# A hybrid decoder step: fetches of the next K block issued one by one on SP, odd sample states in two steps with B masked

## Chip, cores and metric

The kernel runs on one core of a Trainium2 chip. The metric is the device time of one execution in microseconds, the median of several runs. Engines are called PE (matmul), DVE (vector), ACT (scalar), POOL (GpSimd) and SP (sync); PEld is PE's weight load.

## What is computed

One inference step of a two-layer decoder for a prompt of 1024 + 16 positions and 8 samples of 4 positions, 1072 columns in all. Layer 0 is a linear-attention mixer, layer 1 a Mamba-2 mixer; each is followed by a SwiGLU feed-forward (FFN). The parts that the change touches are the FFN, and the new states of the samples in layer 1:

```python
def swiglu(x, w_gate, w_up, w_down):
    return (jax.nn.silu(x @ w_gate) * (x @ w_up)) @ w_down

# ssd_scan, state of one sample: decay, then the sum over its 4 positions
u = jnp.einsum('bnjgrp,bnjgs->bngrps', xdt * decay_end[..., None], bc)
s = chunk_decay[..., None, None] * s + u      # (32 heads x 64) x 128 per sample
```

## The kernel before

**Number format.** Every operand is split in a high and a low part, and a product is three matmuls (wh·xh, wl·xh, wh·xl; `mm3`, lines 229 to 234). Activations lie as 8 rows of 128 features in `xh` and `xl`, 1072 columns each.

**FFN in quads.** Three of the 22 gate/up tiles are done plainly. The other 19 go through `quad_gu`: a two-by-two block product in seven products ("forms" a11, s1, s2, s4, s3, a12, a22), each form 24 matmuls of 268 columns. The results are combined on DVE, split and stored to DRAM tensor `fd` by POOL's queue (`store`, L408 and L409); two quads make a pair, and the second (odd) one combines and stores most. Buffers `t` for this come from a ring of ten. The last quad (number 21) is stored by SP to `oh` and `ol` (`spill`).

The down product (`quad_down`) goes over five K blocks, `DOWN = (2, 2, 2, 2, 1)`. In one block four quads (p = 0 to 3) run over the seven forms; with n = 2 a form is 12 matmuls, so a block is 336. The right operands of a block are 7 forms x n pieces of 536 KB, fetched back from `fd` (L577): forms 0 to 3 into rows of `xh` and `xl` of the block's parity, forms 4 to 6 into strips of the arena (`fo`). The 29 strips of the arena are handed out first in, first out.

**Weights.** `W.pump` keeps up to six forms ready ahead of their use. A raw tile of 512 KB (`raw`, two buffers) comes on SP's queue (L71); a form is summed on DVE where needed (L97), copied high on ACT (L115) and its low part taken on DVE (L116). DVE also adds the finished products into `acc` (L503), in the order of its queue.

**Fetches.** `fetch(c + 1)` stands at the start of block c, all 14 pieces in a row on POOL's queue; block 0 is fetched while quad 21 runs, by the hook `last_gu`. In `quad_gu` and `quad_down` the hook runs before `W.pump(RING)`.

**Samples.** The samples' new states are a side task (`Driver`, `D.add`), stepped between the forms of `quad_gu` at `RATE[7]` = 0.6 steps per form: `even_samples` in layer 0 (32 steps), `odd_samples` in layer 1 (32 states, two steps each). For a state, `odd_samples` loads it on SP (L1533), masks the 512 columns of x for the sample (L1535, DVE), decays the state (L1537, DVE), and one step later multiplies (L1540, PE), adds (L1541, DVE) and stores on SP (L1542). There are two state buffers, halves of one strip. The side task holds four strips until it ends.

A scheduler places the recorded instructions on the engines' queues; within a queue they then run in order.

Of the kernel before, what the change touches and what calls it, by code (L numbers as in the profile page):

```python
# [162 lines left out]
class Core:  # L163
# [247 lines left out]
    def quad_gu(self, W, i, hook=None):  # L411
# [47 lines left out]
        for f in FORMS:  # L459
            w, = W.take(1)  # L460
            for tb in range(2):
                ps = self.product(bank, f, w, self.right, 4, tb)
                if f == "a11":
                    nc.scalar.activation(out=part(keep, 0, tb), in_=ps, func=AF.Copy)
                elif f == "s1":
                    add(part(keep, 2, tb), ps, part(keep, 0, tb))
                elif f == "s2":
                    s2[tb] = self.tmp(Q)
                    add(s2[tb], ps, part(keep, 0, tb))
                elif f == "s4":  # L470
                    sg[tb] = self.tmp(Q)
                    add(sg[tb], ps, s2[tb])
                    nc.scalar.activation(out=sg[tb], in_=sg[tb], func=AF.Silu)
                elif f == "s3":
                    second(ps, tb)
                elif f == "a12":
                    sg[tb] = self.tmp(Q)
                    nc.scalar.activation(out=sg[tb], in_=ps, func=AF.Silu)  # L478
                else:
                    first(ps, tb)  # L480
            self.drop(*w[2])
            if hook:
                hook(f)
            W.pump(RING)
            yield

    def quad_down(self, W, right, n, p, acc, ap1, c, hook=None):
# [7 lines left out]
        for f in FORMS:  # L495
            w, = W.take(1)
            for tb in range(2):
# [4 lines left out]
                else:  # L502
                    nc.vector.tensor_tensor(out=a, in0=a, in1=ps, op=ALU.add)  # L503
            self.drop(*w[2])
            if hook:
                hook(f)
            W.pump(RING)
# [29 lines left out]
    def ffn(self, W, side, order=(0, 1, 2)):  # L537
# [17 lines left out]
                    W.pump(RING)  # L555
        D.drain()
        self.pstags = ["kt", "sc"]
        D.add(self.later, RATE[7])

        nc = self.nc  # L560
        start = [sum(DOWN[:c]) for c in range(len(DOWN))]
        F, own = [[None] * 7 for _ in DOWN], [[] for _ in DOWN]

        def fetch(c, forms=range(7)):


            for f in forms:
                F[c][f] = []
                for j in range(DOWN[c]):
                    if f < 4:  # L570
                        r = 4 * j + f
                        x = (self.xh, self.xl)[r // 4][:, 2 * (r % 4) + c % 2]
                    else:
                        own[c].append(self.strip(F32R, "fo"))
                        x = own[c][-1].t
                    F[c][f].append(x)
# [7 lines left out]

        def last_gu(f):
            if f == "a11":
                fetch(0, range(4))
            elif f == "s2":
                self.drop(*self.T[0], *self.T[1])
                fetch(0, range(4, 7))  # L590

        for i in range(PLAIN, 22):
            yield from self.quad_gu(W, i, last_gu if i == 21 else None)
# [5 lines left out]
        end = len(DOWN) - 1  # L599
        rows = range(1 - end % 2, KD, 2)  # L600
        for c, n in enumerate(DOWN):
            if c < end:
                fetch(c + 1)
            else:
# [494 lines left out]
    def even(self, W, side):  # L1099
# [111 lines left out]
            self.drop(*u)  # L1211
        self.nps = 8
        W.pump(4)
        self.later = self.even_samples(prs)


    def odd_units(self):
# [305 lines left out]
    def odd_samples(self, grs):  # L1523
# [4 lines left out]
        for gr in grs:  # L1528
            g = gr.g
            bs, xs = self.bst(g)  # L1530
            for s in range(8):
                S0 = sp.t[:, (s % 2) * 512:(s % 2) * 512 + 512]
                nc.sync.dma_start(out=S0, in_=I["ss_in"][:, s, 512 * g:512 * g + 512])  # L1533
                xm = self.bxs[2].t[:, 512:1024]
                nc.vector.tensor_scalar(out=xm[:96], in0=xs[:96].bitcast(F32), scalar1=self.onehot[:, s:s + 1],  # L1535
                                        scalar2=None, op0=ALU.mult)
                nc.vector.tensor_tensor(out=v8(S0), in0=v8(S0), in1=gr.cd[:, :, s:s + 1].to_broadcast([P, 8, 64]), op=ALU.mult)  # L1537
                yield
                bu = self.ps(512)
                nc.tensor.matmul(bu, lhsT=bs[:96], rhs=xm[:96], start=True, stop=True)  # L1540
                nc.vector.tensor_tensor(out=S0, in0=S0, in1=bu, op=ALU.add)  # L1541
                nc.sync.dma_start(out=O["ss_s"][:, s, 512 * g:512 * g + 512], in_=S0)  # L1542
                yield
        self.drop(sp, *self.bxs)

    def sgate(self, gr):
# [36 lines left out]
    def odd(self, W, side):  # L1583
# [87 lines left out]
            self.drop(*u)  # L1671
        self.nps = 8
        W.pump(4)
        self.later = self.odd_samples(grs)

    def ffn_units(self, l):
        g, u, d = (self.I[f"{n}{l}"] for n in ("wg", "wu", "wd"))
# [16 lines left out]
ODD0 = 6  # L1694
NPS = 7
START = 6
RATE = [1.2, 1.2, 1.5, 1.5, 1.5, 6.5, 6.0, 0.6, 1.25]


class Driver:  # L1700
# [207 lines left out]
```

## Time and profile before

| | us |
|---|---|
| median of 3 runs | 3062.77 |
| lowest, highest | 3062.67, 3066.0 |
| the profiled execution | 3070.39 |
| its span, first to last instruction | 3068.6 |
| PE busy in the span | 2895.4 (94%) |
| PEld | 2770.4 (90%) |
| DVE | 2246.9 (73%) |
| ACT | 1402.8 (46%) |
| POOL | 360.2 (12%) |

PE's busy share is that of pipelined instructions, so the number of matmuls in a stretch says more than its busy time. In time from the span's start: layer 0 has its gate/up quads from about 680 to 1080 us and the down product to about 1300; layer 1 has them from about 2330 to 2758 and 2758 to 2985.

### The profile page before, as it was taken

To read this page: it belongs to the slowest core of one execution; us is meant where nothing else is said; L and a number is where in the kernel's file an instruction comes from. 1 tells how busy PE (TensorE), PEld (TensorE's weight loads), DVE (VectorE), ACT (ScalarE), POOL (GpSimd) and SP (SyncE) were. 2 spreads that over 40 slices of the span, in tenths; PEclk is the share of its full clock that TensorE was granted. 3 is DMA by queue.
4 is the path that set the end of the run, shared out by engine and by line. 5 is a ranking of instruction groups with operands and counts; after the bars stand their busy time and mean duration, and the time that the engine had idled before them with its cause. 6 is when DMAs were issued, how large, how long until landed. Compare 5 with 4: busy or idle time off the path is not lost. (4 is left out here: it accounts for less than half of the span.)

```text
span 3068.6 us, 54657 instructions
## 1 busy us (share of the span) xinstructions
PE 2895.4 (94%) x20386; PEld 2770.4 (90%) x20386; DVE 2246.9 (73%) x4977; ACT 1402.8 (46%) x3195; POOL 360.2 (12%) x693
## 2 busy tenths in 40 slices
PE   7999999999999988997999999999999999998986
PEld 7998989999899988987889898989999999998986
DVE  7645545687887757897877777775478888874887
ACT  5533435553344442245767575854354343343213
POOL 0000000002333331100000000000001333342100
PEclk9999999999999999998999999999999999999998
DMA  4121226234454485443344445366333655558534
GB/s 137 45 66 35 77 69 203 96 106 148 155 161 143 138 304 222 143 121 102 95 124 129 137 128 135 119 207 211 140 132 112 190 176 171 178 179 316 177 115 129
DMA packets 246267, 442.79 MB, mean 144 GB/s; under 512 B 36177, under 2 KB 172273, under 8 KB 246001
## 3 DMA queue, kind: packets, MB, share of 16 engines
q1 hardware_dynamic: 201360, 292.16, 30.6%
q0 software_dynamic: 44640, 147.14, 13.6%
q8 instruction: 160, 2.62, 0.4%
q14 instruction: 107, 0.87, 0.1%
HBM read 295.12 MB, written 144.07 MB: 143 GB/s over the span
## 5 line engine op out<-in xcount | busy, mean ns | idle before, releaser
L232 PE MATMUL ps<-xh,wh 128*128 128x384 f32 (+1 forms) x2520 | 842.4, 336 | 18.7 <-ACT xh L248 7.6
L233 PE MATMUL ps<-xh,wl 128*128 128x384 f32 (+1 forms) x2520 | 832.5, 331 | 8.6 <-DVE wl L130 8.6
L234 PE MATMUL ps<-xl,wh 128*128 128x384 f32 (+1 forms) x2520 | 832.7, 331 | 0.0
L232 PEld LDWEIGHTS ps<-xh,wh 128*128 128x128 f32 x2520 | 480.5, 191 | 42.2 <-issue 12.3
L233 PEld LDWEIGHTS ps<-xh,wl 128*128 128x128 f32 x2520 | 481.1, 191 | 14.9 <-DVE wl L130 10.2
L234 PEld LDWEIGHTS ps<-xl,wh 128*128 128x128 f32 x2520 | 480.3, 191 | 3.9 <-issue 1.9
L408 POOL DMA_DIRECT2D fd<-t x252 | 137.0, 544 | 1185.8 <-ACT t L248 810.9
L115 ACT ACTIVATE w_s<-sums 128x512 fp32r<-128x512 f32 (+2 forms) x292 | 146.4, 514 | 279.9 <-DVE sums L97 183.7
L115 ACT ACTIVATE w_a<-raw 128x512 fp32r<-128x512 f32 (+2 forms) x214 | 106.8, 515 | 235.4 <-DMA raw<-in_wd 74.5
L232 PE MATMUL qa<-xh,w_a 128*128 128x268 f32 x688 | 200.3, 291 | 5.3 <-ACT t L478 5.0
L130 DVE TENSOR_TENSOR wl<-raw,wh 128x1024 fp32r<-128x1024 f32 (+1 forms) x113 | 138.1, 1223 | 85.2 <-ACT wh L129 71.4
L233 PE MATMUL qa<-xh,w_a 128*128 128x268 f32 x688 | 199.1, 289 | 0.0
L234 PE MATMUL qa<-xl,w_a 128*128 128x268 f32 x672 | 193.7, 288 | 0.0
L248 ACT ACTIVATE t<-t 128x268 fp32r<-128x268 f32 (+2 forms) x230 | 99.8, 438 | 189.2 <-DVE t L419 94.4
L232 PE MATMUL qb<-t,w_s 128*128 128x268 f32 x608 | 174.9, 288 | 9.8 <-DVE t L419 9.8
L233 PE MATMUL qb<-t,w_s 128*128 128x268 f32 x608 | 173.9, 286 | 0.0
L234 PE MATMUL qb<-t,w_s 128*128 128x268 f32 x608 | 173.7, 286 | 0.0
L129 ACT ACTIVATE wh<-raw 128x1024 fp32r<-128x1024 f32 (+1 forms) x113 | 119.3, 1056 | 111.9 <-DMA raw<-in_wd 29.1
L116 DVE TENSOR_TENSOR w_s<-sums,w_s 128x512 fp32r<-128x512 f32 (+2 forms) x292 | 155.8, 544 | 15.8 <-ACT w_s L115 4.0
L97 DVE TENSOR_TENSOR sums<-raw 128x512 f32<-128x512 f32 (+2 forms) x156 | 83.3, 535 | 111.2 <-DMA raw<-in_wd 63.9
L409 POOL DMA_DIRECT2D fd<-t x252 | 137.0, 543 | 34.2 <-DVE t L249 8.9
L116 DVE TENSOR_TENSOR w_a<-raw,w_a 128x512 fp32r<-128x512 f32 (+2 forms) x214 | 116.0, 550 | 32.8 <-ACT w_a L115 27.0
(404 smaller groups left out, 7541.9 us busy)
## 6 DMA issues: line engine op xcount, KB each, us to landing
fd<-t POOLq DMA_DIRECT2D x504, 134.0 KB, 3.0
fo<-fd POOLq DMA_DIRECT2D x54, 536.0 KB, 11.1
raw<-in_wg SPq DMA_DIRECT2D x44, 512.0 KB, 4.0
raw<-in_wu SPq DMA_DIRECT2D x44, 512.0 KB, 4.7
xh<-fd POOLq DMA_DIRECT2D x40, 536.0 KB, 7.2
raw<-in_wd SPq DMA_DIRECT2D x40, 512.0 KB, 4.3
xl<-fd POOLq DMA_DIRECT2D x32, 536.0 KB, 8.8
cumb<-cum_d SPq DMA_DIRECT2D x32, 512.0 KB, 5.7
```

The lines of the kernel that those rows point to most:

```text
L97: nc.vector.tensor_tensor(out=sums[f], in0=x, in1=y, op=op)
L115: nc.scalar.activation(out=tiled(hi), in_=src, func=AF.Copy)
L116: nc.vector.tensor_tensor(out=tiled(lo), in0=src, in1=tiled(hi).bitcast(F32), op=ALU.subtract)
L129: c.nc.scalar.activation(out=hi.t[:, :w], in_=r, func=AF.Copy)
L130: c.nc.vector.tensor_tensor(out=lo.t[:, :w], in0=r, in1=hi.t[:, :w].bitcast(F32), op=ALU.subtract)
L232: nc.tensor.matmul(out, lhsT=wh, rhs=xh, start=first, stop=False, **kw)
L233: nc.tensor.matmul(out, lhsT=wl, rhs=xh, start=False, stop=False, **kw)
L234: nc.tensor.matmul(out, lhsT=wh, rhs=xl, start=False, stop=last, **kw)
L248: self.nc.scalar.activation(out=hi, in_=src, func=AF.Copy)
L408: self.nc.gpsimd.dma_start(out=self.fd[:, i, FORMS.index(f), o:o + Q], in_=hi.bitcast(F32))
L409: self.nc.gpsimd.dma_start(out=self.fd[:, i, FORMS.index(f), 2 * Q + o:2 * Q + o + Q], in_=lo.bitcast(F32))
```

## The change

1. In `quad_gu` and `quad_down` `W.pump(RING)` now stands ahead of the hook.
2. `fetch` issues one piece on SP's queue (`nc.sync`) in place of POOL's. In block c a hook `paced` runs after every form and issues one piece of block c + 1 every second form (every fourth where the next block has seven pieces; in the last block one pair of plain rows every seventh). For block 0 the first eight pieces still go out at once after form a11 of quad 21, the other six after s2.
3. `even_samples` are stepped at 0.3 per form, `odd_samples` at 0.55.
4. `odd_samples` loads the state and masks B (128 columns in four slots) one step ahead of its product; decay, addition and store come a step later. Load and store are on POOL's queue.

```diff
@@ quad_gu and quad_down
             self.drop(*w[2])
+            W.pump(RING)
             if hook:
                 hook(f)
-            W.pump(RING)
             yield
@@ ffn
-        D.add(self.later, RATE[7])
+        D.add(*self.later)
...
+        pieces = lambda c: [(f, j) for f in range(7) for j in range(DOWN[c])]
...
-                    nc.gpsimd.dma_start(out=x.bitcast(F32), in_=self.fd[:, start[c] + j, f])
+            nc.sync.dma_start(out=x.bitcast(F32), in_=self.fd[:, start[c] + j, f])
+
+        def fetch_plain(i):
+            for dst, src in ((self.xh, self.oh), (self.xl, self.ol)):
+                nc.sync.dma_start(out=dst[:, rows[i]].bitcast(F32), in_=src[:, i])
...
         for c, n in enumerate(DOWN):
-            if c < end:
-                fetch(c + 1)
-            else:
-                for i, r in enumerate(rows):
-                    for dst, src in ((self.xh, self.oh), (self.xl, self.ol)):
-                        nc.gpsimd.dma_start(out=dst[:, r].bitcast(F32), in_=src[:, i])
+            todo = [(fetch, c + 1, *x) for x in pieces(c + 1)] if c < end else [(fetch_plain, i) for i in range(PLAIN + 1)]
+            every, count = 4 * 7 // len(todo), [0]
+
+            def paced(f):
+                count[0] += 1
+                if todo and count[0] % every == 0:
+                    fn, *args = todo.pop(0)
+                    fn(*args)
+
             for p in range(4):
-                yield from self.quad_down(W, right(c), n, p, acc, ap1, c)
+                yield from self.quad_down(W, right(c), n, p, acc, ap1, c, paced)
             self.drop(*own[c])
@@ odd_samples
+        masked = lambda i: self.bxs[2].t[:, 512 + (i % 4) * P:512 + (i % 4) * P + P]
+        def load(i):
+            gr, s = steps[i]
+            nc.gpsimd.dma_start(out=state(i), in_=I["ss_in"][:, s, 512 * gr.g:512 * gr.g + 512])
+            nc.vector.tensor_scalar(out=masked(i)[:96], in0=self.bst(gr.g)[0][:96].bitcast(F32),
+                                    scalar1=self.onehot[:, s:s + 1], scalar2=None, op0=ALU.mult)
+        def product(i):
+            bu[i] = self.ps(512)
+            nc.tensor.matmul(bu[i], lhsT=masked(i)[:96], rhs=self.bst(steps[i][0].g)[1][:96], start=True, stop=True)
+        load(0)
+        yield
+        for i, (gr, s) in enumerate(steps):
+            S0 = state(i)
+            if i + 1 < len(steps):
+                load(i + 1)
+            product(i)
+            yield
+            nc.vector.tensor_tensor(out=v8(S0), in0=v8(S0), in1=gr.cd[:, :, s:s + 1].to_broadcast([P, 8, 64]), op=ALU.mult)
+            nc.vector.tensor_tensor(out=S0, in0=S0, in1=bu[i], op=ALU.add)
+            nc.gpsimd.dma_start(out=O["ss_s"][:, s, 512 * gr.g:512 * gr.g + 512], in_=S0)
+            yield
@@
-RATE = [1.2, 1.2, 1.5, 1.5, 1.5, 6.5, 6.0, 0.6, 1.25]
+RATE = [1.2, 1.2, 1.5, 1.5, 1.5, 6.5, 6.0, 0.3, 1.25, 0.55]
```

**SP in the down product of layer 1.** Before, from the stores of the last gate/up quad (`oh`, `ol`) on, with `raw` the raw weight tiles:

```order
L627 DMA ol<-t 128x268
L71 DMA raw<-in_wd 128x4x256
L626 DMA oh<-t 128x268
L627 DMA ol<-t 128x268
L71 DMA raw<-in_wd 128x4x256 x13
L71 DMA raw<-in_wd 128x2x256 x4
```

In the change, on the same queue, from the raw tile of quad p = 2 of block 0 on:

```order
L71 DMA raw<-in_wd 128x4x256
L577 DMA xh<-fd 128x1072
L577 DMA xl<-fd 128x1072
L577 DMA xh<-fd 128x1072
L71 DMA raw<-in_wd 128x4x256
L577 DMA xl<-fd 128x1072
L577 DMA xh<-fd 128x1072
L577 DMA xl<-fd 128x1072
L577 DMA xh<-fd 128x1072
L71 DMA raw<-in_wd 128x4x256
L577 DMA xl<-fd 128x1072
L577 DMA fo<-fd 128x1072 x2
```

The pieces that stood on POOL's queue now stand on SP's, three or four between two raw tiles.

**The sample states of layer 1.** Before, their loads (`ssm<-in_ss_in`) and stores (`out_ss_s<-ssm`) stand on SP among the raw gate and up tiles:

```order
L1533 DMA ssm<-in_ss_in 128x512
L1542 DMA out_ss_s<-ssm 128x512
L1533 DMA ssm<-in_ss_in 128x512
L71 DMA raw<-in_wg 128x1024
L71 DMA raw<-in_wu 128x1024
L1542 DMA out_ss_s<-ssm 128x512
```

In the change they stand on POOL, among the stores of the quads' results (L408, L409):

```order
L1560 DMA out_ss_s<-ssm 128x512
L408 DMA fd<-t 128x268
L409 DMA fd<-t 128x268
L408 DMA fd<-t 128x268
L409 DMA fd<-t 128x268
L1542 DMA ssm<-in_ss_in 128x512
L408 DMA fd<-t 128x268 x2
L409 DMA fd<-t 128x268 x2
L1560 DMA out_ss_s<-ssm 128x512
L1542 DMA ssm<-in_ss_in 128x512
```

They moved from the weights' queue to that of the results; a load stands right behind the store of the state before it, or some results later.

**DVE in the gate/up quads of layer 1.** Before, with the mask (L1535), the decay (L1537) and the addition (L1541) of a sample state among the quad's own work:

```order
L1541 TENSOR_TENSOR ssm<-ssm,ps 128x512
L419 TENSOR_TENSOR hraw<-hraw,t 128x268
L116 TENSOR_TENSOR w_s_27451<-sums,w_s_27451 128x512
L1535 TENSOR_SCALAR bxs<-bxs,c_onehot 96x512
L116 TENSOR_TENSOR w_s_27487<-sums,w_s_27487 128x512
```

In the change, in a like place:

```order
L1558 TENSOR_TENSOR ssm<-ssm,cd_19874 128x512
L419 TENSOR_TENSOR t<-qb,keep 128x268
L97 TENSOR_TENSOR sums<-raw 128x512
L97 TENSOR_TENSOR sums<-sums,raw 128x512
L419 TENSOR_TENSOR t<-qb,keep 128x268
L116 TENSOR_TENSOR w_s_27959<-sums,w_s_27959 128x512
L1559 TENSOR_TENSOR ssm<-ssm,ps 128x512
L419 TENSOR_TENSOR t<-qe,t 128x268
L97 TENSOR_TENSOR sums<-raw,sums 128x512
L1543 TENSOR_SCALAR bxs<-bxs,c_onehot 96x128
```

The mask is now 96x128, and decay and addition follow each other within one step.

## Rows read from the trace of the kernel before

**Rows 1.** busy us (instructions) of each engine by stretch, columns in its first line

```profile
core 0: us, PE busy (x) PEld busy (x) DVE busy (x) ACT busy (x) POOL busy (x), PEclk, DMA share, GB/s
2770.00:2780.00 10.00, 4.21 (x32) 3.78 (x31) 0.00 (x0) 0.00 (x0) 3.24 (x6) 0.89 1.04 411
2780.00:2800.00 20.00, 16.91 (x119) 16.91 (x120) 10.15 (x29) 10.30 (x29) 3.25 (x6) 0.80 0.96 372
2800.00:2820.00 20.00, 20.00 (x164) 20.00 (x164) 10.90 (x29) 10.41 (x31) 5.96 (x11) 1.00 0.56 196
2820.00:2840.00 20.00, 15.02 (x110) 14.81 (x109) 12.26 (x36) 3.67 (x10) 1.62 (x3) 0.91 0.70 268
2840.00:2860.00 20.00, 20.00 (x165) 20.00 (x164) 18.03 (x50) 4.94 (x14) 1.96 (x4) 1.00 0.22 64
2860.00:2880.00 20.00, 15.84 (x128) 15.65 (x127) 11.95 (x33) 3.88 (x11) 5.62 (x11) 1.00 1.03 388
```

**Rows 2.** the same view, three stretches of layer 0

```profile
1100.00:1120.00 20.00, 11.28 (x74) 10.30 (x73) 7.43 (x22) 5.88 (x17) 6.56 (x13) 0.80 1.04 412
1160.00:1180.00 20.00, 15.84 (x111) 15.63 (x110) 14.54 (x40) 4.07 (x11) 0.00 (x0) 0.83 0.47 173
1200.00:1220.00 20.00, 16.04 (x118) 15.85 (x117) 13.83 (x41) 4.65 (x12) 2.19 (x5) 0.91 0.82 312
```

**Rows 3.** chain that ended last, 2756 to 2870: start, us, what

```profile
2765.97 14.18 DMA raw<-in_wd
...
2865.93 12.08 DMA raw<-in_wd
```

**Rows 4.** timeline of DVE: start, us, instruction, idle time before it

```profile
2780.25 0.42 DVE L97 TENSOR_TENSOR sums<-raw 128x256 f32<-128x256 f32 x1 [10.71 <-DMA raw<-in_wd]
```

**Rows 5.** DMA queues, 2758 to 2800: packets, MB, share of 16 engines

```profile
q0 software_dynamic: 3621, 13.76, 81.2%
q1 hardware_dynamic: 2736, 2.67, 18.3%
```

**Rows 6.** the view of rows 1, where SP alone issues large fetches

```profile
2052.00:2056.00 4.00, 4.00 (x24) 3.34 (x22) 1.43 (x3) 3.95 (x11) 0.00 (x0) 1.00 1.07 388
```

**Rows 7.** page, part 6: DMA issues over the whole span

```profile
fd<-t POOLq DMA_DIRECT2D x504, 134.0 KB, 3.0
...
raw<-in_wd SPq DMA_DIRECT2D x40, 512.0 KB, 4.3
```

**Rows 8.** that view: layer 0 with samples, without, layer 1 with

```profile
680.00:880.00 200.00, 184.67 (x1447) 181.51 (x1446) 164.79 (x332) 75.08 (x169) 60.63 (x112) 0.99 0.49 157
880.00:1060.00 180.00, 180.00 (x1455) 179.58 (x1454) 146.70 (x317) 77.36 (x173) 63.04 (x117) 1.00 0.46 142
2320.00:2700.00 380.00, 356.68 (x2781) 349.50 (x2779) 320.90 (x688) 148.50 (x330) 114.86 (x212) 1.00 0.53 170
```

**Rows 9.** that view: an odd unit of layer 0 without samples

```profile
950.00:960.00 10.00, 10.00 (x82) 9.90 (x81) 9.81 (x25) 6.25 (x15) 7.06 (x13) 1.00 0.60 181
```

**Rows 10.** waits of PE, 2320 to 2758: us in total, times, longest

```profile
PE qb L232 <- DVE t L419: 19.5, 15, 2.0
```

**Rows 11.** groups of DVE instructions, 2320 to 2758: busy us, mean ns, idle

```profile
L1537 DVE TENSOR_TENSOR ssm<-ssm,cd 128x512 f32<-128x512 f32 x32 | 22.0, 688 | 11.7 <-DMA ssm<-in_ss_in 11.5
L1541 DVE TENSOR_TENSOR ssm<-ssm,ps 128x512 f32<-128x512 f32 x32 | 21.7, 678 | 0.0
L1535 DVE TENSOR_SCALAR bxs<-bxs,c_onehot 96x512 fp32r<-96x512 f32 x31 | 14.8, 476 | 0.0
```

**Rows 12.** DMA issues, 2320 to 2758, columns as above

```profile
ssm<-in_ss_in SPq DMA_DIRECT2D x32, 256.0 KB, 2.8
out_ss_s<-ssm SPq DMA_DIRECT2D x32, 256.0 KB, 2.2
```

**Rows 13.** page, part 5: busy us, mean ns, idle before

```profile
L408 POOL DMA_DIRECT2D fd<-t x252 | 137.0, 544 | 1185.8 <-ACT t L248 810.9
```

**Rows 14.** waits, 2320 to 2740

```profile
DVE t L249 <- DMA fd<-t: 6.4, 8, 1.5
```

More of the change, by code (lines that the diff above doesn't have):

```diff
@@ L504, in quad_down @@
             self.drop(*w[2])
+            W.pump(RING)
             if hook:
                 hook(f)
-            W.pump(RING)
             yield
@@ L557, in ffn, with fetch @@
         self.pstags = ["kt", "sc"]
-        D.add(self.later, RATE[7])
+        D.add(*self.later)
         nc = self.nc
         start = [sum(DOWN[:c]) for c in range(len(DOWN))]
[L562 to L572, printed above, removed]
-                    else:
-                        own[c].append(self.strip(F32R, "fo"))
-                        x = own[c][-1].t
-                    F[c][f].append(x)
-                    nc.gpsimd.dma_start(out=x.bitcast(F32), in_=self.fd[:, start[c] + j, f])
+        F, own = [[[] for _ in range(7)] for _ in DOWN], [[] for _ in DOWN]
+        end = len(DOWN) - 1
+        rows = range(1 - end % 2, KD, 2)
+        pieces = lambda c: [(f, j) for f in range(7) for j in range(DOWN[c])]
+        def fetch(c, f, j):
+            if f < 4:
+                r = 4 * j + f
+                x = (self.xh, self.xl)[r // 4][:, 2 * (r % 4) + c % 2]
+            else:
+                own[c].append(self.strip(F32R, "fo"))
+                x = own[c][-1].t
+            F[c][f].append(x)
+            nc.sync.dma_start(out=x.bitcast(F32), in_=self.fd[:, start[c] + j, f])
+        def fetch_plain(i):
+            for dst, src in ((self.xh, self.oh), (self.xl, self.ol)):
+                nc.sync.dma_start(out=dst[:, rows[i]].bitcast(F32), in_=src[:, i])
         def right(c):
@@ L586, in last_gu @@
             if f == "a11":
-                fetch(0, range(4))
+                for f, j in pieces(0)[:8]:
+                    fetch(0, f, j)
             elif f == "s2":
                 self.drop(*self.T[0], *self.T[1])
-                fetch(0, range(4, 7))
+                for f, j in pieces(0)[8:]:
+                    fetch(0, f, j)
         for i in range(PLAIN, 22):
@@ L598, in ffn @@
         ap1 = [self.strip(F32, "ap1") for _ in range(2)]
-        end = len(DOWN) - 1
-        rows = range(1 - end % 2, KD, 2)
         for c, n in enumerate(DOWN):
-            if c < end:
-                fetch(c + 1)
-            else:
-                for i, r in enumerate(rows):
-                    for dst, src in ((self.xh, self.oh), (self.xl, self.ol)):
-                        nc.gpsimd.dma_start(out=dst[:, r].bitcast(F32), in_=src[:, i])
+            todo = [(fetch, c + 1, *x) for x in pieces(c + 1)] if c < end else [(fetch_plain, i) for i in range(PLAIN + 1)]
[5 more added lines that the diff above has]
+                    fn(*args)
             for p in range(4):
-                yield from self.quad_down(W, right(c), n, p, acc, ap1, c)
+                yield from self.quad_down(W, right(c), n, p, acc, ap1, c, paced)
             self.drop(*own[c])
@@ L1213, in even @@
         W.pump(4)
-        self.later = self.even_samples(prs)
+        self.later = self.even_samples(prs), RATE[7]
     def odd_units(self):
@@ L1527, in odd_samples @@
         v8 = lambda a: a.rearrange("p (h d) -> p h d", h=8)
[L1528 to L1543, printed above, removed]
+        steps = [(gr, s) for gr in grs for s in range(8)]
+        state = lambda i: sp.t[:, (i % 2) * 512:(i % 2) * 512 + 512]
+        masked = lambda i: self.bxs[2].t[:, 512 + (i % 4) * P:512 + (i % 4) * P + P]
+        bu = [None] * len(steps)
+        def load(i):
[18 more added lines that the diff above has]
+            yield
         self.drop(sp, *self.bxs)
@@ L1673, in odd @@
         W.pump(4)
-        self.later = self.odd_samples(grs)
+        self.later = self.odd_samples(grs), RATE[9]
     def ffn_units(self, l):
```

## The prediction

> **What bounds the kernel now.** PE does, nearly everywhere: busy 94% of the span. So I looked for stretches in which PE does fewer matmuls than its full pace, and asked what it waited for there. I read the busy time by stretch first, then the chain that ended last, then the DMA queues of the worst stretch, then the groups and waits of the gate/up stage.
>
> *Down product.* Full pace is 164 matmuls in 20 us (the stretch from 2800 in [rows 1]), 8.2 per us. Layer 1 falls short by 50 in the ten us from 2770, by 45 from 2780, by 54 from 2820 and by 36 from 2860: 185 matmuls, 22.6 us. Layer 0 falls short by 90, 53 and 46 [rows 2]: 189, or 23.0 us. Together 45.6 us. Part of each loss is idle PE, part a lower granted clock behind the stop (0.89 and 0.80 in [rows 1]). The chain says who is late: a raw weight tile, 14.18 and 12.08 us from issue to landing [rows 3], where the median is 4.3 [rows 7]. DVE stood 10.71 us in front of a sum for it [rows 4]; the additions of finished products queue behind that sum on DVE, so PE's banks are not freed and PE stops. Why the tile is late: the DMA engines were full (403 to 412 GB/s in the bad stretches of [rows 1, 2]), and 13.76 MB of 16.4 were the fetches and stores on POOL's queue, which took 81.2% of the time; SP's queue got 18.3% [rows 5]. All pieces of a block go out at once, and the weights starve for some 20 us.
>
> *Gate/up quads.* Layer 0 without samples does 1455 matmuls in 180 us, 8.08 per us, PE never idle. With samples it does 1447 in 200 us [rows 8]: 170 short, 21 us; 2 us of that are the 16 sample products themselves (one long matmul is worth about two short ones), so 19 us are stalls. Layer 1 does 2781 in 380 us: 291 short, 36 us; about 4 are the 32 sample products and an estimated 3 the longer matmuls of plain tiles at its start, so 29 us are stalls. PE waits there for DVE's reading of a bank, 19.5 us in 15 waits [rows 10]. DVE is the cause: an odd unit holds it 9.81 us of ten even without samples [rows 9].
>
> **The change, part by part.** Sums are against the profiled execution, 3070.39 us (span 3068.6 and 1.8 around it). The median of the runs is 3062.77, so at the end I scale by 3062.77/3070.39 = 0.9975.
>
> *Fetches on SP, spaced.* A block of 336 matmuls lasts 41.0 us at full pace, a form 1.46 us. It needs 14 pieces of 0.549 MB and 4 raw tiles of 0.524 MB: 9.8 MB, 239 GB/s, where SP's queue alone has moved 388 [rows 6]. Bandwidth suffices, if the weights get theirs in time. At 388 GB/s a piece takes 1.41 us. What stands before a raw tile on SP is now three or four pieces, by the order shown ahead. SP does not space these itself: it issues them as soon as their buffers are free. But the tile in front of them waits for DVE to free its raw buffer, once per quad (10.2 us), so a group of four goes out at once, takes 5.6 us, and is through before the next tile is issued. That tile then lands in about 4.3 us. It is needed seven to eight forms after its issue (10.2 to 11.7 us): it is issued when the a22 form of its buffer's quad is made, six forms ahead of PE. Even a tile that stands right behind four pieces lands within 5.6 + 4.3 = 9.9 us. So I expect the stalls to go, apart from the start of block 0, where 14 pieces and eight stores stand before the tile for p = 2. There the fetch begins right after PE's a11 of quad 21, no longer behind POOL's own stores, but so it now runs beside quad 20's stores, whose `t` buffers come back later. I leave 3 us per layer for that: of 45.6 us, 40 go. The ends are 15 (a late tile in each quad, below) and 45. What is late next is DVE: at PE's full pace it is busy 18.03 us of 20 in block 1 (the stretch from 2840 in [rows 1]), so it can follow, with little to spare. Strips give no wait: a `fo` strip handed out was last read some eight forms earlier. POOL loses 126 issues and nobody waited for POOL's time there. `W.pump` ahead of the hook puts a raw tile ahead of a piece: at most one piece, 1.41 us, on a path with slack, taken as nothing.
>
> *Samples of layer 1.* DVE spent 22.0 + 21.7 + 14.8 us on them and stood 11.7 us for the loads [rows 11]: 70 us. The new mask has a quarter of the columns: between 119 ns (a quarter of 476) and 476; I take 250, near the middle. That is 32 x (688 + 678 + 250) ns = 52 us, and the load, issued one step (1.8 forms, 5.3 us) ahead, lands in 2.8 us [rows 12], so the wait goes. 52 for 70 us: if stalls follow DVE's load, 29 x 18/70 = 7 us go; if only load beyond some slack stalls PE, all 29. Since DVE has almost no slack in an odd unit [rows 9] I stay near the low end and take 8, and 3 more because SP no longer waits for sample data in front of raw tiles.
>
> *POOL takes the samples' DMAs.* 64 more issues of 0.54 us [rows 13] stand among the results' stores. A load waits until the store before it in the same buffer has landed (2.2 us, [rows 12]; 3.0 for POOL's own, [rows 7]), and the results queued behind it hold their `t` buffers; DVE already waits 6.4 us for these [rows 14]. Nothing, if each falls between stores; up to 31 x (2.2 + 1.1) = 102 us if every one holds all. Mostly the load stands with no ready store behind it. I take 5 us: half of 1.1 us in each of nine odd units.
>
> *Samples of layer 0.* Same work over twice the time. Proportional stalls: 0 gained; stalls from excess alone: up to 19. I take 3. Their four strips are held 55 forms longer, which costs a form of lead that is hidden now.
>
> Sum: -40 - 8 - 3 + 5 - 3 = -49. 3070.4 - 49 = 3021.4, times 0.9975: **3014 us**.
>
> **Rivals.** *Gate/up stalls mostly vanish.* Half the sample density in layer 0 and a third less in layer 1 stay under DVE's room: 43 + 22 + 10 = 75 us gone, 2995, scaled 2988. For it: without samples there is no stall at all [rows 8]. Against: 9.81 of ten.
>
> *The spacing isn't one.* Since only a raw tile's wait holds SP, a group goes out at once, and a tile may land 9.9 us after issue plus some 2 us by which DVE lags. Against a lead of 10.2 to 11.7 that is late by 0 to 2 us in each of the 28 quads of full blocks: 28 x 1.1 = 31 of the 45.6 us stay. With 9 from the samples: 3070.4 - 24 = 3046, scaled 3039. For it: the fetch is as large as before. The Trainium skill ("DMA: Bandwidth & Descriptors", section "Queues, rings and completion order") says that a DMA engine takes turns between queue rows packet by packet, and that on one row descriptors start in order. By that rule the move costs the weights the turns of a row of their own, which is what this rival prices; the trace shows how little those turns gave, 18.3% [rows 5]. The same page, section "Issuing engines are not separate DMA queues", says that issuing from another engine saves only the time to issue. By that, the queue alone would change nothing (3063), and all of the gain lies in the spacing; the full DMA engines in [rows 1] agree.
>
> *Slower: POOL is held.* In layer 1's gate/up quads a sample load waits on POOL for the landing of a store, results queue behind it, the ten `t` buffers run out, and DVE and then PE stop. With the share s of the 102 us that reaches PE the sum is -54 + 102 s: break-even at s = 0.53, slower than the median by over 0.2% from s = 0.59, and 3111 at s = 1. For it: [rows 14], and loads that stand directly behind a store. Against: where load and store are neighbours, the results behind them belong to later forms.
>
> **How the numbers follow.** Forecast (3014) 0.58; stalls vanish (2988) 0.14; no real spacing (3039) 0.15; POOL held 0.13, of which 0.05 within 0.2% and 0.08 slower. 0.2% (6 us) is about what a measurement of this kernel can tell from no change. Faster 0.87, same 0.05, slower 0.08. The range reaches to both faster cases, with the end of the down term (15 for 40 gives 3039) and a little beyond: 2988 to 3044.
>
> **What would show it.** Right: the down product lasts some 20 us less per layer, raw tiles land in 4 to 7 us there, no stretch of 20 us under 155 matmuls in blocks 1 to 3. Layer 1's gate/up stage: DVE's groups of the samples fall to 52 us, no wait for `ssm`. Wrong: DVE still waiting over 5 us for a raw tile in the down product; DVE or ACT waiting for `t` behind POOL by over 30 us; PE stalls in layer 0 that run on for twice as long at the same size.

## The result and the profile after

| | us |
|---|---|
| before, median of 4 runs | 3062.72 |
| after, median of 4 runs | 3032.78 (3031.77 to 3037.73) |
| ratio after / before | 0.990, 95% interval 0.989 to 0.992 |
| span of the profiled execution after | 3031.6 |

The forecast was 3014, its range 2988 to 3044. The time lies in the range, on the side that was given 0.87, but the gain is 30 us where 49 were forecast. The next table tells where it came from and where some of it went, in one trace of each kernel (3068.6 and 3031.6 us long, so 37 us apart where the medians differ by 30). The stages are worked out from first and last starts in each trace: the first `keep` copy of a layer's quads (L464) begins gate/up, the first copy into `acc` or `ap` (L501) the down product, and the last addition of `ap` (L514) ends it.

| stage, us | before | after | difference |
|---|---|---|---|
| up to layer 0's gate/up quads | 681.5 | 675.2 | -6.3 |
| layer 0, gate/up quads | 417.9 | 420.9 | +3.0 |
| layer 0, down product | 232.1 | 203.2 | -28.9 |
| between | 1001.5 | 999.9 | -1.6 |
| layer 1, gate/up quads | 432.9 | 460.8 | +27.9 |
| layer 1, down product | 233.1 | 201.6 | -31.5 |
| behind it | 69.6 | 70.0 | +0.4 |

The down products gained 60 us. Layer 1's gate/up quads gave 28 back. The first line isn't the change's doing: over all traces of this study that stretch took 671 to 682 us, whatever the kernel.

The down product of layer 1 after, by stretch, in the columns of [rows 1]:

```profile
2760.00:2780.00 20.00, 20.00 (x165) 20.00 (x163) 11.73 (x33) 11.97 (x35) 0.00 (x0) 1.00 1.02 367
2780.00:2800.00 20.00, 20.00 (x164) 20.00 (x163) 10.12 (x29) 11.24 (x33) 0.00 (x0) 1.00 0.80 292
2800.00:2820.00 20.00, 20.00 (x164) 20.00 (x164) 19.47 (x54) 6.81 (x19) 0.00 (x0) 1.00 0.93 329
...
2840.00:2860.00 20.00, 20.00 (x164) 20.00 (x163) 19.45 (x57) 6.10 (x18) 0.00 (x0) 1.00 0.88 313
```

PE does its full 164 matmuls in each stretch, at clock 1.00. The DMA engines still are full in the first (1.02 of their time), as in [rows 1], and PE loses nothing by it. DVE is busy up to 19.47 us of 20 and follows.

The DMA queues in the stretch of [rows 5], 2758 to 2800, and under them the issues: count, size, median us from issue to landing.

```profile
q1 hardware_dynamic: 6466, 13.94, 91.2%
...
xh<-fd SPq DMA_DIRECT2D x6, 536.0 KB, 7.0
fo<-fd SPq DMA_DIRECT2D x6, 536.0 KB, 8.7
xl<-fd SPq DMA_DIRECT2D x5, 536.0 KB, 9.3
raw<-in_wd SPq DMA_DIRECT2D x5, 512.0 KB, 7.5
```

13.94 MB go through in the 42 us, where two rows moved 16.43 before, and they do so in one row. A raw tile lands in 7.5 us at the median; in the same view of the kernel before it took 10.9 us (three tiles), and [rows 3] had 14.18 and 12.08.

Layer 1's gate/up stage after, 380 us as in the last line of [rows 8]:

```profile
2290.00:2670.00 380.00, 349.12 (x2669) 339.94 (x2668) 297.19 (x646) 140.88 (x313) 143.07 (x263) 0.98 0.49 159
```

2669 matmuls where [rows 8] has 2781. DVE is busy less (297 us for 321), and yet PE gets less done. The groups of DVE's sample instructions in 2290 to 2770 (busy us, mean ns, idle before) answer to [rows 11]:

```profile
L1558 DVE TENSOR_TENSOR ssm<-ssm,cd 128x512 f32<-128x512 f32 x32 | 22.1, 691 | 50.4 <-DMA ssm<-in_ss_in 50.4
L1559 DVE TENSOR_TENSOR ssm<-ssm,ps 128x512 f32<-128x512 f32 x32 | 21.8, 680 | 0.4 <-PE ps L1548 0.4
L1543 DVE TENSOR_SCALAR bxs<-bxs,c_onehot 96x128 fp32r<-96x128 f32 x28 | 7.8, 277 | 0.0
```

The work shrank to 52 us, as forecast. The wait for the state's load, which was to go, rose from 11.5 to 50.4 us. Timeline of POOL and of DVE after, start, us, instruction, idle time before it:

```profile
2611.48 0.68 DVE L1559 TENSOR_TENSOR ssm<-ssm,ps 128x512 f32<-128x512 f32 x1
...
2623.40 0.69 DVE L1558 TENSOR_TENSOR ssm<-ssm,cd 128x512 f32<-128x512 f32 x1 [3.93 <-DMA ssm<-in_ss_in]
...
2627.45 0.68 DVE L1559 TENSOR_TENSOR ssm<-ssm,ps 128x512 f32<-128x512 f32 x1
```

```profile
2613.87 0.54 POOL L1560 DMA_DIRECT2D out_ss_s<-ssm  x1
...
2620.50 0.55 POOL L1542 DMA_DIRECT2D ssm<-in_ss_in  x1 [3.48 <-DMA out_ss_s<-ssm]
```

The state added at 2611.48 is stored at 2613.87. There are two state buffers, so the load of the state after next waits for this store to land and goes out at 2620.50; and from 2619.47 on (3.93 us before 2623.40) DVE stands in front of the decay of exactly that state, which starts when the load has landed. In the code the decay stands directly ahead of its own addition, three steps behind the load. But the decay needs nothing from PE, and in the trace it stands on DVE's queue ahead of the addition of the sample before. (That the scheduler takes the load to be there by then is an inference; its reckoning is in no trace.) So the lead that the code gives is taken back, and all of DVE's later work stands behind a load that has just been issued. PE pays by waiting for DVE's reading of a bank (waits in 2290 to 2770: us, times, longest; [rows 10] had 19.5):

```profile
PE qb L232 <- DVE t L419: 33.1, 22, 3.6
```

### The profile page after: what moved, and what is told of

It is laid out like the page before. It is cut to its first block, busy times and chain, and to the rows that moved or that the text cites. A ratio compares the mean times of both kernels' runs of the same rounds, so it can differ in the third digit from the quotient of the medians.

```text
span 3031.6 us, 54611 instructions
## 1 busy us (share of the span) xinstructions
PE 2881.8 (95%) x20386; PEld 2754.1 (91%) x20386; DVE 2242.1 (74%) x4977; ACT 1407.2 (46%) x3195; POOL 318.2 (10%) x615
## 4 chain that ended last, share of the span: by engine, by line
PE 41%; issue 14%; DVE 8%; POOL 6%; DMA 5%; ACT 2%; POOLq 0%; SPq 0%; DVEq 0%; ACTq 0%
PE ps L232 8%; PE ps L233 8%; PE ps L234 8%; POOL fd L409 3%; POOL fd L408 3%; PE qb L233 2%; PE qb L232 2%; PE qb L234 2%; DMA cumb<-cum_d 2%; PE qa L232 1%; PE qe L232 1%; PE qe L234 1%; PE qe L233 1%; PE qa L233 1%; PE qa L234 1%
## 5 line engine op out<-in xcount | busy, mean ns | idle before, releaser
L115 ACT ACTIVATE w_s<-sums 128x512 fp32r<-128x512 f32 (+2 forms) x292 | 147.3, 514 | 278.7 <-DVE sums L97 216.1
L408 POOL DMA_DIRECT2D fd<-t x252 | 137.0, 543 | 647.5 <-ACT t L248 619.6
L115 ACT ACTIVATE w_a<-raw 128x512 fp32r<-128x512 f32 (+2 forms) x214 | 107.3, 516 | 154.4 <-PE qb L234 52.5
L232 PEld LDWEIGHTS qa<-xh,w_a 128*128 128x128 f32 x688 | 132.4, 192 | 20.1 <-ACT t L478 19.2
L409 POOL DMA_DIRECT2D fd<-t x252 | 137.0, 543 | 25.2 <-DVE t L249 4.8
```

The lines of the kernel that those rows point to most:

```text
L115: nc.scalar.activation(out=tiled(hi), in_=src, func=AF.Copy)
L232: nc.tensor.matmul(out, lhsT=wh, rhs=xh, start=first, stop=False, **kw)
L408: self.nc.gpsimd.dma_start(out=self.fd[:, i, FORMS.index(f), o:o + Q], in_=hi.bitcast(F32))
L409: self.nc.gpsimd.dma_start(out=self.fd[:, i, FORMS.index(f), 2 * Q + o:2 * Q + o + Q], in_=lo.bitcast(F32))
```

## Experiments

The first four take the change apart, the next four try the cause of the loss, two the cause of the gain, and one is an attempt at more. All are compared with the kernel before, run on the same chip beside them: e1 to e4, e5 to e8 and e9 to e11 ran on three chips, where the kernel before took 3067.7, 3066.7 and 3061.4 us, so between these groups the ratios are compared and not the times. The edits shown are against the changed kernel for e1, e5 and e6, against the kernel before for e2, against e1 for e3, e4 and e8 to e10, and against e7 for e11; for e7 the text says it. Stages and waits come from one trace of each kernel. "Tiles" is the time that ACT (L115) and DVE (L97) together waited for raw tiles of the down product in the whole span, given where the fetches are in question; "down" is both layers' down products, "g/u 1" layer 1's gate/up quads.

| kernel | median us | ratio to before (95%) | down | g/u 1 | tiles |
|---|---|---|---|---|---|
| before | | 1 | 465.2 | 432.9 | 138.4 |
| after | 3032.8 | 0.990 (0.989, 0.992) | 404.8 | 460.8 | 32.6 |
| e1 fetches alone | 3010.8 | 0.981 (0.979, 0.983) | 405.2 | 432.7 | 43.8 |
| e2 samples alone | 3086.6 | 1.006 (1.004, 1.008) | 467.2 | 453.4 | |
| e3 as e1, pieces on POOL | 3081.0 | 1.005 (1.003, 1.006) | 480.9 | 430.7 | 100.8 |
| e4 as e1, pieces at once | 3007.4 | 0.980 (0.979, 0.982) | 405.0 | 431.8 | 39.4 |
| e5 after, decay late | 3005.4 | 0.980 (0.977, 0.983) | 403.2 | 426.7 | |
| e6 after, loads on SP | 3028.9 | 0.988 (0.984, 0.991) | 404.8 | 454.2 | |
| e7 e5, samples' DMAs on SP | 2998.0 | 0.979 (0.976, 0.982) | 405.1 | 430.1 | |
| e8 as e1, B masked | 3010.6 | 0.982 (0.980, 0.985) | 405.0 | 435.6 | |
| e9 as e1, raw tiles on POOL | 3056.8 | 0.999 (0.998, 1.000) | 441.3 | 439.0 | 69.7 |
| e10 as e1, both on POOL | 3018.1 | 0.986 (0.984, 0.988) | 415.3 | 433.9 | 51.6 |
| e11 after, decay on POOL, DMAs on SP | 3012.0 | 0.984 (0.982, 0.986) | 406.0 | 443.9 | |

**e1, the fetches alone.** `odd_samples` and the rates are those of before.

```diff
-RATE = [1.2, 1.2, 1.5, 1.5, 1.5, 6.5, 6.0, 0.3, 1.25, 0.55]
+RATE = [1.2, 1.2, 1.5, 1.5, 1.5, 6.5, 6.0, 0.6, 1.25, 0.6]
 def odd_samples(self, grs):
...
```

> Only the fetches of the down product are changed (one by one, on SP's queue, and raw tiles ahead of pieces); the sample states of both layers are as before. Theory A: the spacing alone gains what the down stage showed, 29 + 32 us, and the new form of the samples loses 28 us in layer 1's gate/up quads and 3 us in layer 0's. So this kernel takes about 3003 us, with layer 1's gate/up stage near 433 us and layer 0's near 418. Theory B: the fetches themselves take time from the gate/up quads (those of block 0 begin there, and POOL's and SP's stores share the DMA engines), and the samples cost nothing: then it takes about 3033 us as the whole change does.

3010.8 us. Down products 405 us and layer 1's gate/up quads 432.7 us, both as theory A had them; B falls. Layer 0's gate/up quads take 420.0 us at 0.6 steps per form, where the whole change takes 420.9 at 0.3: the slower rate moved nothing that a trace can tell. e1 also has `W.pump` ahead of the hook, and so have e3 and e4; that part was not tried by itself, but with the pieces on POOL (e3) it gains nothing.

**e2, the samples alone.** `quad_gu`, `quad_down` and `ffn` are those of before.

```diff
-        D.add(self.later, RATE[7])
+        D.add(*self.later)
 def odd_samples(self, grs):
...
```

> Only the samples are changed (B masked, one step ahead, DMAs on POOL, rates 0.3 and 0.55); the fetches of the down product go out on POOL's queue at the start of a block, as before. Theory A: slower than before by the 28 + 3 us that the gate/up stages lost, about 3094 us. Theory B: no loss of their own, about 3063 us. By the forecast's own terms (-8 -3 +5 -3) it would be 3054 us.

Slower than before, by 0.6%: theory A's sign, with 18 us where it had 31. Layer 1's gate/up quads lost 20.5 us here and 27.9 in the whole change. Where the other 7 us come from, when both parts are in, stays open.

**e3, the same places in the code, but POOL's queue.**

```diff
-            nc.sync.dma_start(out=x.bitcast(F32), in_=self.fd[:, start[c] + j, f])
+            nc.gpsimd.dma_start(out=x.bitcast(F32), in_=self.fd[:, start[c] + j, f])
...
-                nc.sync.dma_start(out=dst[:, rows[i]].bitcast(F32), in_=src[:, i])
+                nc.gpsimd.dma_start(out=dst[:, rows[i]].bitcast(F32), in_=src[:, i])
```

> As e1, but the pieces are issued on POOL's queue at the same places of the code. If the places in the code space the pieces, and the queue makes no difference, it takes what e1 takes, about 3003 us. If it is SP's row that spaces them, because there the pieces stand behind raw tiles that wait for a buffer, POOL runs ahead, the eight pieces of a block whose space is free go out at once as before, and most of the stall comes back: 3040 to 3063 us, with raw tiles of the down product landing in over 10 us.

3081 us, slower than before and beyond the 3040 to 3063 expected for this case. The gain is gone with the queue. DMA queues of e3 in 2758 to 2800, and the landing of raw tiles:

```profile
q0 software_dynamic: 3207, 12.18, 73.5%
q1 hardware_dynamic: 2736, 2.67, 18.6%
...
raw<-in_wd SPq DMA_DIRECT2D x3, 512.0 KB, 13.1
```

The shares are nearly those of [rows 5]. They are also nearly the rows' shares of the bytes (2.67 of 14.85 MB is 18.0%; in [rows 5] it is 16.3%), so they only say how much each row was asked to move, and not that SP's row was held back. That shows in the landing, 13.1 us, and in what stood in front of the tile (ACT's timeline and PE's waits of e3, the latter in 2735 to 2990):

```profile
2764.10 0.38 ACT L501 ACTIVATE ap<-qa 128x268 f32<-128x268 f32 x1
2775.45 0.42 ACT L115 ACTIVATE w_a<-raw 128x256 fp32r<-128x256 f32 x1 [10.98 <-DMA raw<-in_wd]
2775.78 0.38 ACT L501 ACTIVATE ap<-qa 128x268 f32<-128x268 f32 x1
...
PE qe L232 <- ACT acc L501: 9.1, 1, 9.1
```

ACT waits 10.98 us for a tile, the copies of finished products (L501) queue behind it, and PE waits 9.1 us for a bank. This is the mechanism of the prediction, with ACT in DVE's place. And POOL doesn't keep the spacing of the code, as its timeline shows:

```profile
2807.65 0.54 POOL L577 DMA_DIRECT2D xh<-fd  x1 [5.03 <-PE qa L234]
2808.34 0.54 POOL L577 DMA_DIRECT2D fo<-fd  x1
...
2813.03 0.54 POOL L577 DMA_DIRECT2D xl<-fd  x1 [0.39 <-PE qb L234]
2829.70 0.55 POOL L577 DMA_DIRECT2D fo<-fd  x1 [16.13 <-PE qe L234]
```

Nine pieces go out in 5.4 us, then POOL waits 16.13 us for PE to free a strip. That it ends behind the kernel before, with less waiting for tiles (100.8 for 138.4 us), may come from such pieces that start late; this wasn't tried.

**e4, SP's queue, all pieces at once.**

```diff
-                if todo and count[0] % every == 0:
+                while todo and count[0] == 1:
```

> As e1, on SP's queue, but all pieces of a block are issued one after the other behind its first form. If moving to the weights' queue is what helps, it takes e1's time, about 3003 us. If the spacing helps, the next raw tile stands behind 14 pieces of 1.41 us, 20 us, and lands some 24 us after its turn where about 10.5 us are to spare: some 13 us lost in each of six full blocks that fetch, so 3003 + 6 x 13 = 3081 us, or with half of it hidden 3040.

3007.4 us, the same as e1 within the intervals. So the spacing in the code is worth nothing that shows; the price expected for its absence, 13 us in each of six blocks, was wrong. Issues of e4 in 2765 to 2805:

```profile
fo<-fd SPq DMA_DIRECT2D x6, 536.0 KB, 10.9
raw<-in_wd SPq DMA_DIRECT2D x5, 512.0 KB, 5.3
```

The pieces get late here, 10.9 us at the median, and they have a block's time, 41 us, for it. But the medians hide that single tiles get late too: behind a burst they take up to 11.9 us (below, under e9), nearly as long as the 12.08 of [rows 3], and the down product doesn't suffer. What ACT waited for them is less (whole span: us, times, longest; e3's line first, then e4's):

```profile
ACT w_a L115 <- DMA raw<-in_wd: 86.0, 15, 11.0
ACT w_a L115 <- DMA raw<-in_wd: 32.2, 11, 6.3
```

**e5, the decay placed late.** One dependency more, without a semaphore: on DVE the decay comes behind its product on PE.

```diff
-            nc.tensor.matmul(bu[i], lhsT=masked(i)[:96], rhs=self.bst(steps[i][0].g)[1][:96], start=True, stop=True)
+            mm[i] = nc.tensor.matmul(bu[i], lhsT=masked(i)[:96], rhs=self.bst(steps[i][0].g)[1][:96], start=True, stop=True)
...
-            nc.vector.tensor_tensor(out=v8(S0), in0=v8(S0), in1=gr.cd[:, :, s:s + 1].to_broadcast([P, 8, 64]), op=ALU.mult)
+            dec = nc.vector.tensor_tensor(out=v8(S0), in0=v8(S0), in1=gr.cd[:, :, s:s + 1].to_broadcast([P, 8, 64]), op=ALU.mult)
+            self.tc.add_manual_dep(dec.ins, mm[i].ins.name, mybir.DependencyInfo(
+                mybir.DependencyClass.NoSync, mybir.DependencyReason.DATA), reason="decay")
```

> The changed kernel with one thing more: on DVE the decay of a sample's state is placed behind its product on TensorE, so that it stands directly ahead of its addition instead of one sample ahead. Theory C: layer 1's gate/up quads lost 28 us because DVE stands in front of the decay until the state's load has landed (48.7 us in the trace of the changed kernel); placed later, the load has had a whole sample more. Then the wait falls under 10 us, the stage from 460.8 to about 433 us, and the kernel takes 3033 - 28 = 3005 us. Theory D: what costs is the samples' DMAs on POOL, behind which the results wait and hold their buffers; then it takes 3033 us as before, with the stage at 455 us or more.

3005.4 us; layer 1's gate/up quads take 426.7 us. Waits of e5 in 2290 to 2770:

```profile
POOL ssm L1542 <- DMA out_ss_s<-ssm: 57.7, 21, 5.6
...
PE qb L232 <- DVE t L419: 11.1, 10, 2.5
...
DVE ssm L1558 <- DMA ssm<-in_ss_in: 1.2, 1, 1.2
```

DVE's wait fell from 50.4 to 1.2 us and PE's from 33.1 to 11.1, and the stage by 34 us. POOL's waiting is what it was, 57.7 us for 58.1 in the whole change. So the loss came from where the decay stands on DVE, and not from the results held behind POOL: theory C holds, and D falls.

**e6, only the loads on SP.**

```diff
-            nc.gpsimd.dma_start(out=state(i), in_=I["ss_in"][:, s, 512 * gr.g:512 * gr.g + 512])
+            nc.sync.dma_start(out=state(i), in_=I["ss_in"][:, s, 512 * gr.g:512 * gr.g + 512])
```

> The changed kernel with the loads of the sample states on SP's queue; their stores stay on POOL's, and the decay stays where it is. Theory C (the decay stands too early, right after the state buffer's own store): the load still waits for that store to land, so at least half of the wait stays, 25 us or more, and the kernel takes 3019 to 3033 us. Theory D (POOL's order): the results no longer stand behind a load that waits, and the whole loss goes: about 3005 us.

3028.9 us, within theory C's bounds. The wait stays, since the load still waits for the store (waits in 2290 to 2770):

```profile
DVE ssm L1558 <- DMA ssm<-in_ss_in: 36.7, 21, 3.7
```

**e7, the decay late and both DMAs on SP.** The edits of e5 and e6, and the store on SP too.

```diff
-            nc.gpsimd.dma_start(out=O["ss_s"][:, s, 512 * gr.g:512 * gr.g + 512], in_=S0)
+            nc.sync.dma_start(out=O["ss_s"][:, s, 512 * gr.g:512 * gr.g + 512], in_=S0)
```

> The changed kernel with the decay directly ahead of its addition and all DMAs of layer 1's samples on SP's queue. Theory C: as with the late decay alone, 3005 us within 5. Theory D: 3005 us too; together with the two other runs it tells whether both are needed. If either order on SP holds up raw tiles of the weights, it is slower than the late decay alone, by the waits for raw tiles that it adds.

2998.0 us, the lowest median of the study, faster than both kernels, and 2 us below the 3005 within 5 that was expected. Against e5 the intervals overlap, and in the traces layer 1's gate/up quads are no shorter (430.1 us for 426.7); 8.8 us of the difference lie ahead of layer 0's gate/up quads (671.0 us for 679.8), which no edit touches. Nothing shows that SP's queue adds to the late decay.

**e8, B masked, all else as e1.**

```diff
-                xm = self.bxs[2].t[:, 512:1024]
-                nc.vector.tensor_scalar(out=xm[:96], in0=xs[:96].bitcast(F32), scalar1=self.onehot[:, s:s + 1],
+                bm = self.bxs[2].t[:, 512 + (s % 4) * P:512 + (s % 4) * P + P]
+                nc.vector.tensor_scalar(out=bm[:96], in0=bs[:96].bitcast(F32), scalar1=self.onehot[:, s:s + 1],
...
-                nc.tensor.matmul(bu, lhsT=bs[:96], rhs=xm[:96], start=True, stop=True)
+                nc.tensor.matmul(bu, lhsT=bm[:96], rhs=xs[:96], start=True, stop=True)
```

> As e1 (only the fetches changed), but B is masked in place of the inputs; order, rate and queue of the samples are as before. 32 masks of 277 ns instead of 477 ns take 6.4 us off DVE. If PE's stalls in layer 1's gate/up quads follow DVE's load, 2.5 to 6.4 us go: about 3004 to 3008 us where e1 takes 3010. If they follow something else, no difference.

3010.6 us, by the ratios no difference from e1. But the intervals are some 8 us wide on either side, and 2.5 to 6.4 us were in question: whether PE's stalls follow 6.4 us of DVE's work isn't settled by this run.

**e9, the roles of the queues exchanged.** Pieces on SP, raw tiles of the down quads on POOL.

```diff
-            c.nc.sync.dma_start(out=out, in_=src)
+            (c.nc.gpsimd if len(src.shape) == 3 else c.nc.sync).dma_start(out=out, in_=src)
```

> As e1 (pieces one by one on SP's queue), but the raw weight tiles of the down product's quads go out on POOL's queue: two rows again, with the roles exchanged. Theory E: what ends the stalls is that tiles and pieces stand in one row, in the order of the code, so that a tile has at most the pieces before it ahead of it; two rows compete again and the stalls come back, 3060 to 3085 us as before and in e3. Theory F: POOL's row simply gets the larger share of the DMA engines (73 to 81% of their time against 18% for SP's in the stretches of before and e3), and it harmed because the pieces had it; then the tiles on POOL's row land early and the kernel takes e1's time, 3005 to 3011 us.

3056.8 us, within 0.3% of before and 3 us under theory E's 3060: two rows again, and the gain of e1 is gone but for 0.1%. The down product loses 36 us against e1. Queues of e9 in 2758 to 2800, and the landing of its tiles there:

```profile
q1 hardware_dynamic: 3800, 11.15, 69.4%
q0 software_dynamic: 456, 1.61, 12.1%
...
raw<-in_wd POOLq DMA_DIRECT2D x3, 512.0 KB, 6.3
```

POOL's row now carries the tiles. Its 12.1% is again its share of the bytes (1.61 of 12.76 MB, 12.6%). Theory F's time is refuted, since the kernel is slow. But half of what F said came out: on POOL's row the tiles land soon, in 6.3 us where e3 had 13.1. Landings of all tiles in e9, in e4 and in the kernel before, shortest, median, longest:

```profile
DMA to landing us min/median/max: 3.0/4.0/9.0
DMA to landing us min/median/max: 2.6/4.1/11.9
DMA to landing us min/median/max: 2.6/4.1/14.7
```

In e9 no tile takes over 9.0 us, and the down products lose 36 us; in e4 some take 11.9, and nothing is lost. So a late landing alone is not the loss. Between these two kernels it goes with how long ACT and DVE stand in front of a tile, 69.7 us in e9 and 39.4 in e4. That depends on the order in which they got their work, too, and the order is not the same in these kernels. The tile for quad p = 2 of block 0 in layer 1 goes out as follows in e1, e3 and e9, where the down product starts at 2732.2, 2764.1 and 2766.4:

```profile
2736.26 0.39 SPq L71 DMA_DIRECT2D raw<-in_wd  x1
2751.03 0.37 SPq L71 DMA_DIRECT2D raw<-in_wd  x1
2751.65 0.76 POOL L71 DMA_DIRECT2D raw<-in_wd  x1 [3.80 <-DVE sums L97]
```

That is 4 us behind the start in e1, and 13 and 15 us ahead of it in e3 and e9. So an edit that moves only the queue in the code also moves when a tile goes out. In the kernel before it goes out with the start, at 2765.97 for 2765.9, much as in e1, but lands 14.18 us later [rows 3] where e1 has 4.1: there the late landing is what differs. How much of the loss of e3 and e9 is landing and how much the order on ACT and DVE wasn't tried and stays open. The stretch 2760 to 2780 of e9, columns of [rows 1], shows the same picture as [rows 1], and the clock below 1.00 with it:

```profile
2760.00:2780.00 20.00, 16.41 (x118) 16.04 (x118) 13.16 (x37) 10.06 (x29) 1.52 (x2) 0.91 0.88 320
```

**e10, tiles and pieces both on POOL.** The edits of e3 and e9 together:

```diff
-            c.nc.sync.dma_start(out=out, in_=src)
+            (c.nc.gpsimd if len(src.shape) == 3 else c.nc.sync).dma_start(out=out, in_=src)
...
+            nc.gpsimd.dma_start(out=x.bitcast(F32), in_=self.fd[:, start[c] + j, f])
```

> As e1, but raw tiles of the down product's quads and pieces both go out on POOL's queue, in the order of the code; SP's queue issues neither. Theory E (one row is what matters) and theory F: as e1, 3005 to 3011 us. Theory G (a piece or a tile issued from POOL is late in itself, whatever stands on the other row): slow again, 3060 us or more, as e3.

3018.1 us, near e1, 39 us below e9. Tiles and pieces stand in one row again, and theory G falls: issuing from POOL is not slow in itself. By the ratios it stays 14 us behind e1, and it is 7 us over the bound expected, with waits for tiles of 51.6 us for 43.8. What else POOL's row costs wasn't followed.

**e11, the decay on POOL.** e7 without its dependency, and:

```diff
-            nc.vector.tensor_tensor(out=v8(S0), in0=v8(S0), in1=gr.cd[:, :, s:s + 1].to_broadcast([P, 8, 64]), op=ALU.mult)
+            nc.gpsimd.tensor_tensor(out=v8(S0), in0=v8(S0), in1=gr.cd[:, :, s:s + 1].to_broadcast([P, 8, 64]), op=ALU.mult)
```

> An attempt at a faster version: the changed kernel with all DMAs of layer 1's samples on SP's queue, and the decay of the state on POOL instead of DVE. It takes 32 x 0.69 = 22 us off DVE, and what waits for the load is POOL, not DVE. If PE's remaining stalls in layer 1's gate/up quads follow DVE's load, 10 to 20 us go against the late decay on SP's queue (2998 us): 2978 to 2990. If POOL takes several times as long for it, or the waiting decay holds the results' stores behind it and with them their buffers, it is slower: 3005 us or more.

3012.0 us, by the ratios no gain over e7. Group of POOL in 2290 to 2770:

```profile
L1558 POOL TENSOR_TENSOR ssm<-ssm,cd 128x512 f32<-128x512 f32 x32 | 37.2, 1165 | 470.1 <-DMA ssm<-in_ss_in 469.9
```

POOL takes 1165 ns for what DVE does in 691, and now POOL stands in front of the load (373 of the 470 us are the wait for the first one). The stage takes 443.9 us. That the results behind it are what costs wasn't shown.

## Why the prediction was right, and where it was wrong

*The down product.* Where the loss sat and what PE waited for was read rightly from [rows 1, 3 and 4], and it went. Two readings beside it were not right: the 18.3% of [rows 5] is about SP's share of the bytes and no sign of starving, and the DMA engines were not full in all seven of the worst stretches (0.47, 0.70 and 0.82 in three of them; of the 403 to 412 GB/s named, only 411 and 412 stand in the rows). The size was off: -40 forecast, -60 measured. The 45.6 us had been added up over the seven worst stretches alone, and then were taken as the upper bound; the rest of the stage also ran a little below its pace. Counting the stage as a whole (232 us against 41.0 us for each full block) would have shown it. The 3 us per layer for the start of block 0 weren't needed either: the stretch from 2760 has its 165 matmuls. Raw tiles were to land in 4 to 7 us; they took 7.5 in the stretch shown, and PE didn't suffer.

*Why it went.* The forecast put the gain on the spacing. That step failed: e4 has no spacing in the code and gains the same, and e3 has it, on POOL's queue, and gains nothing. What the change does is to put the pieces into the row of the tiles: in the kernels with one row the down products take 403 to 415 us, in the four with two rows (before, e2, e3, e9) 441 to 481. Tiles on a row of their own beside the pieces on POOL's took up to 14.7 us to land, in one row up to 10.1 (11.9 with bursts). e4 and e9 show that this is not all of it: what counts is whether ACT or DVE stands in front of a tile that hasn't landed, and their order differs between these kernels. From the kernel before to e1 the order at the start of the stage hardly moves and the landing does (14.18 us to 4.1 for the same tile), so there the landing is the likelier cause; for e3 and e9 the shares of the two stay open.

The Trainium skill was weighed at this place. By the Trainium skill ("DMA: Bandwidth & Descriptors", section "Issuing engines are not separate DMA queues"), issuing from several engines saves only the time to issue; by that alone the move would change nothing, 3063 us. The runs differ: e3 against e1 and e9 against e10 change the queue alone in the code, and are 70 and 39 us apart. The Trainium skill's other section on that page, "Queues, rings and completion order", says that a DMA engine takes turns between the rows that have work, packet by packet, and starts the descriptors of one row in order. Longest landings of 9.9 us in e1 and 14.5 in e3 agree with it; the loss of e9, where no tile takes over 9.0 us, it doesn't explain. The prediction had drawn from it that the tiles lose the turns of a row of their own, and had priced that as a loss; moving into one row was a gain.

*The rival without spacing* (3039) is refuted as a mechanism by e4, though 3032.8 lies near its number. It counted 28 quads of full blocks; two layers of four such blocks have 32.

*Samples of layer 1.* Forecast -8 and -3, for DVE's load and for SP; measured together with POOL's term +28. DVE's time fell to 52 us as forecast (the mask 277 ns where 250 was taken). The step that failed is "the load, issued one step ahead, lands in 2.8 us, so the wait goes". It looked at where the load is issued, and not at where the decay stands on DVE's queue. Nor did it count here that with two buffers the load can't go out before the store of the state before it in the same buffer has landed, a wait that it had put into POOL's term alone. e5 moves the decay alone and takes 34 us off the stage. Of the two gains forecast none was seen; e8 is too coarse to tell whether stalls of PE follow 6.4 us of DVE's work.

*POOL takes the samples' DMAs.* +5 was forecast. POOL did wait 58 us for the stores' landing, but in e5 it waits as long, and the stage is 34 us shorter. The rival "POOL is held" had the right wait, for the store of a state, but the wrong victim: DVE stood in front of the load itself; results without a buffer were not what stopped it.

*Samples of layer 0.* -3 was forecast; e1 at 0.6 and after at 0.3 differ by 0.9 us: no gain.

So the sum hit the range by luck: one term was 20 us too small as a gain, and others made a loss of 28 us where a gain of 6 was forecast. Errors of opposite sign, of 20 and 34 us, cancelled in part.

## What to carry to other kernels

When a small transfer that somebody waits for competes with bulk transfers, try it in their queue as well as on one of its own; here the one queue was worth 39 and 70 us, whether SP or POOL issued it. Judge it by who stands in front of the transfer and for how long, and not by its landing or by a queue's share of the DMA engines alone. And where a load is moved ahead, look at the order in which the consumer's engine got its instructions: here an operation that depends on the load alone came early, and DVE, which works in order, stood in front of it with all its other work; a dependency on the step that really comes before it put it back.

## What was not expected of the hardware

A row's share of the DMA engines' time was close to its share of the bytes whichever engine issued what: SP's 18.3% for 16.3% of the bytes before and 18.6% for 18.0% in e3, POOL's 12.1% for 12.6% in e9. The same raw tiles go in packets of another size by the engine that issues them. Two tiles of 512 KB each, issued by SP in the kernel before (2841 to 2858) and by POOL in e9 (2874 to 2886), packets and MB:

```profile
q1 hardware_dynamic: 1056, 1.05, 19.0%
q0 software_dynamic: 288, 1.05, 26.1%
```

That is about 1 KB a packet from SP and 3.6 KB from POOL, so e9 is not e3 with the roles merely exchanged. Whether this is why its tiles land sooner wasn't tried. POOL's product of two 128x512 operands took 1165 ns where DVE's took 691. And the stretch up to layer 0's gate/up quads took between 671 and 682 us in the traces, a spread of 11 us that no edit explains; a difference of a few us between two single traces means nothing here.
